# MLA queries of a two-layer decoder step in six projection tiles instead of eight, with the rotary halves in tiles of their own

## The chip, the cores and the metric

One program on 1 core of a Trainium2 chip. The metric is device microseconds of that core for the whole step, both layers; lower is better.

## The reference

One inference step of a two-layer decoder for 256 prompt tokens (one sequence) and 64 sample tokens (8 sequences of 8, each with 2048 cached positions). All is kept feature-major: 128 features on the partitions, the 320 tokens along the row. Per layer:

```
x += 0.5 * SwiGLU(RMSNorm(x))
x += W_out [HGRN2 | RWKV-7 | MLA](RMSNorm(x) @ W_in)
x += 0.5 * SwiGLU(RMSNorm(x))
```

The change touches the MLA queries:

```python
q = (rms_norm(qa, W['mla_q_norm'][l]) @ W['mla_wqb'][l]).reshape(B, T, MLA_HEADS, MLA_NOPE + MLA_ROPE)
q_nope = q[..., :MLA_NOPE]                 # 64 of 96 columns of each of 8 heads
q_pe = rope(q[..., MLA_NOPE:], pos)        # 32 columns, two halves of 16:
                                           # [x1*cos - x2*sin, x2*cos + x1*sin]
c = rms_norm(kva, W['mla_kv_norm'][l])
k_pe = rope(kpe[:, :, None, :], pos)[:, :, 0]
# prompt: scores = q_nope . (c wuk) + q_pe . k_pe
# sample: q_lat = einsum('bqhd,rhd->bqhr', q_nope, wuk); scores = q_lat . c_past + q_pe . kpe_past
```

## The kernel before

Every dense product runs in a split form of fp32: a weight block of 128x128 becomes a rounded high part and a remainder, the moving data too, and `dense_steps` (line 396) issues three matmuls of 320 columns for each block (high x high, high x low, low x high). The weights of a mixer come as one stream of blocks, four to a transfer (`raw`, 256 KB, 4 buffers); `block` (line 382) casts the high part on ACT (line 427) and makes the remainder on DVE (line 428), into three pairs of `w` buffers.

In a layer's mixer, `mla_in` (line 641) projects six tiles: three of the query's low rank, one with the rotary key, two of the latent. It squares the query tiles, sums them over the partitions with a matmul against ones, and takes the root on ACT and the reciprocal on DVE (lines 450 and 451): `rq`. Multiplied by the table `cs` of cosines and sines (with 64 rows of ones on top) that is `csq` (line 671). `mla_q` (line 703) then makes one tile of 128 rows for each of 8 heads: 64 plain rows, 32 rotary rows, and the same 32 with their halves swapped. Two DVE operations take a tile out of PSUM times `csq`: `qS` (64 sample columns, line 721) and `qT` (256 prompt columns, line 722). The matmul over 128 rows then adds rotary and swapped rows by itself, since the key stands twice in `kpe` and `kT`; for the samples line 731 adds them. `absorb` (line 711) multiplies a head's 64 plain rows by `wukt`, three matmuls of 64 columns, and ACT copies the result into `qlat` (line 716), which the sample scores read.

PSUM has 8 banks under four names with a fixed number of buffers each, taken in turn:

```python
BANKS = {"pd": 2, "pr": 3, "pa": 2, "pv": 1}
for h in range(NH):
    ps = self.bank(("pd", "pr", "pr", "pd", "pr")[h % 5])[:, :T]
```

The order of the instructions on each engine comes from the framework's scheduler, which lays the program out by a model of time; `high_priority` moves a part forward. After the queries the mixer weaves three streams (RWKV and HGRN2 recurrences, the attention over cached pages, dense tiles) by a running estimate of TensorE's time. Page tiles (`ct`, `cn`) are fetched on SP's queue, between the weight transfers.

Of the kernel before, what the change touches and what calls it, by code (L numbers as in the profile page):

```python
# [25 lines left out]
NH = 8  # L26
# [72 lines left out]

# [30 lines left out]
def _constants():  # L130
# [11 lines left out]
    r["cs"] = np.concatenate([np.ones((64, T), f), c, c, -s, s], 0).astype(f)  # L142
# [60 lines left out]
def _pack(i):  # L203
# [16 lines left out]
    a["wukt"] = np.concatenate([wukt, np.zeros_like(wukt[..., :32])], 3).reshape(L, 64, NH * 3 * KR)  # L220
# [36 lines left out]
class Kern:  # L257
# [383 lines left out]
    def mla_in(self, xh, xl):  # L641
        nc, l = self.nc, self.l
        self.mark(f"mla_in{l}")
        cs = self.a([128, T], "cs")
        self.wukt = self.a([64, NH, 3 * KR], "wukt")
# [7 lines left out]
        with self.tc.issue_after(self.raws[-1]):  # L653
            nc.sync.dma_start(cs, self.ap["cs"])
# [5 lines left out]
        for j in range(6):  # L660
# [5 lines left out]
            if j == 4:  # L666
                pq = self.bank("pa")[:, :T]
                self.mm(pq, self.c("ones"), accq, start=True, stop=True)
                rq = self.rstd_from(pq, self.ta, "rq", 1.0 / 384)
                self.csq = self.a([128, T], "csq")  # L670
                nc.vector.tensor_tensor(out=self.csq, in0=cs, in1=rq, op=ALU.mult)
            if j < 3:
                qa = self.a([128, T], "qa")
                nc.vector.tensor_tensor(out=qa, in0=ps, in1=self.rstd, op=ALU.mult)
                self.sumsq(qa, accq, j == 0)
                self.split_scaled(qa, self.v(l, "gq", j), self.qh[:, j, :], self.ql[:, j, :])
            elif j == 3:
                csr = self.a([128, T], "qa")
                nc.vector.tensor_tensor(out=csr, in0=cs, in1=self.rstd, op=ALU.mult)
# [3 lines left out]
                for r in (64, 96):  # L683
                    nc.vector.tensor_tensor(out=self.kpe[r:r + 32], in0=t1[64:96], in1=t1[96:128], op=ALU.add)
# [6 lines left out]
    def mla_c(self):  # L691
# [3 lines left out]
        rk = self.rstd_from(ps[:, :T], self.ta, "rq", 1.0 / 256)  # L695
# [7 lines left out]
    def mla_q(self):  # L703


        nc = self.nc
        self.mark(f"mla_q{self.l}")
        self.qT = self.b([128, NH, TP], "qT")
        q = self.a([128, NH, TS], "qS")

        def absorb(h):
            pl = self.bank("pa")
            for kt in range(3):
                self.mm(pl[:KR, kt * 64:kt * 64 + 64], self.wukt[:, h, kt * KR:kt * KR + KR], q[0:64, h, :],
                        start=True, stop=True)
            nc.scalar.copy(self.qlat[:KR, :, :, h, :], pl[:KR, :192].rearrange("p (r s t) -> p r s t", r=3, t=8))

        for h in range(NH):
            ps = self.bank(("pd", "pr", "pr", "pd", "pr")[h % 5])[:, :T]
            self.dense(ps, 3, self.tiles(self.qh, 3), self.tiles(self.ql, 3))  # L720
            nc.vector.tensor_tensor(out=q[:, h, :], in0=ps[:, TP:], in1=self.csq[:, TP:], op=ALU.mult)
            nc.vector.tensor_tensor(out=self.qT[:, h, :], in0=ps[:, :TP], in1=self.csq[:, :TP], op=ALU.mult)
            if h == 4:
                self.mla_c()
            if h > 1:
                absorb(h - 2)
        absorb(6)
        absorb(7)

        sp = lambda x: x.rearrange("p h (s t) -> p s h t", t=8)  # L730
        nc.vector.tensor_tensor(out=self.qlat[64:96, 2], in0=sp(q[64:96]), in1=sp(q[96:128]), op=ALU.add)


    def prompt(self):
# [9 lines left out]
        kT = self.b([128, NH, TP], "kT")  # L744
        for h in range(0, NH, 4):
            nc.gpsimd.tensor_copy(kT[64:128, h:h + 4, :], self.kpe[64:128, None, :TP].to_broadcast([64, 4, TP]))
# [788 lines left out]
```

## Time and profile before

| what | value |
|---|---|
| median of 3 runs | 1675.93 us (1675.06 to 1678.35) |
| the profiled execution's own time | 1670.47 us |
| its span, first to last instruction | 1668.5 us |
| PE busy | 1625.2 us, 97% of the span |
| DVE busy | 955.0 us, 57% |
| ACT busy | 716.6 us, 43% |
| POOL busy | 80.2 us, 5% |
| mean granted TensorE clock | 0.988 |
| bytes moved by DMA | 260.05 MB, mean 156 GB/s |

PE's matmuls are pipelined, so a row of the timeline is longer than the distance to the next row; what a matmul costs in a row of its kind is that distance. A bracket at the end of a timeline row is the idle time before it and what ended it. In the first layer the MLA part lies at 250 to 294 us, in the second at 1073 to 1116 us.

### The profile page before, as it was taken

The numbers are of one execution on the slowest core, as the hardware profiler recorded it, in microseconds if no ns is written. First come the engines' busy times: TensorE is split into PE (matmuls) and PEld (weight loads), VectorE is DVE, ScalarE is ACT, GpSimd is POOL, SyncE is SP. The second block draws the span as 40 slices with busy tenths as digits, with TensorE's granted clock in tenths as the row PEclk, the third lists the DMA queues.
The fourth block names the chain that finished last, engine by engine and source line by source line (L and its number), as shares of the span: only waits on it lengthen the run. The fifth ranks groups of instructions, "written<-read, shape, count | busy, mean of one in ns | idle before, by whom it ended". The sixth has DMA issues, their size and how long they took to land.

```text
span 1668.5 us, 33401 instructions
## 1 busy us (share of the span) xinstructions
PE 1625.2 (97%) x13174; PEld 1449.8 (87%) x13174; DVE 955.0 (57%) x1599; ACT 716.6 (43%) x1208; POOL 80.2 (5%) x112
## 2 busy tenths in 40 slices
PE   8999999999989899999999999999999999999998
PEld 8999998777657599999999999987766676999997
DVE  7555447854446585554465554478335565755543
ACT  6444334633343364443344443346233543544432
POOL 0000000200022000000000000002000310000000
PEclk9999999999999999999999999999999999999999
DMA  8555526646564465555545555366357644555442
GB/s 282 152 150 147 149 86 170 184 143 180 155 209 138 133 209 152 152 152 149 148 146 152 152 151 148 105 175 189 109 157 208 189 134 132 159 152 150 149 148 91
DMA packets 130908, 260.05 MB, mean 156 GB/s; under 512 B 17264, under 2 KB 75952, under 8 KB 130624
## 3 DMA queue, kind: packets, MB, share of 16 engines
q1 hardware_dynamic: 119072, 237.21, 48.0%
q10 hardware_dynamic: 11648, 20.65, 4.1%
q8 instruction: 104, 1.70, 0.4%
q0 software_dynamic: 32, 0.07, 0.1%
q14 instruction: 52, 0.43, 0.1%
HBM read 253.39 MB, written 4.47 MB: 155 GB/s over the span
## 4 chain that ended last, share of the span: by engine, by line
PE 65%; DVE 2%; DMA 2%; ACT 1%; SPq 1%; issue 1%; DVEq 0%; ACTq 0%
PE pd L286 25%; PE pr L286 23%; PE pa L286 14%; PE pv L286 3%; PE pa L290 1%; DMA cn<-in_cn 1%; ACT S L903 0%; DMA ct<-in_ct 0%; DVE w L428 0%; DMA raw<-in_wm 0%; SPq L874 0%; PE pd L290 0%; SPq L917 0%; SPq L854 0%; ACT L903 0%
## 5 line engine op out<-in xcount | busy, mean ns | idle before, releaser
L428 DVE TENSOR_TENSOR w<-raw,w 128x1024 fp32r<-128x1024 f32 (+1 forms) x392 | 410.9, 1051 | 321.4 <-ACT w L427 308.9
L427 ACT CAST w<-raw 128x1024 fp32r<-128x1024 f32 (+1 forms) x392 | 354.7, 909 | 425.0 <-PE pd L286 203.1
L286 PE MATMUL pd<-xh,w 128*128 128x320 f32 x1792 | 425.2, 316 | 7.7 <-ACT w L427 6.8
L286 PEld LDWEIGHTS pd<-xh,w 128*128 128x128 f32 x1792 | 305.6, 190 | 24.2 <-issue 9.7
L286 PE MATMUL pd<-xl,w 128*128 128x320 f32 x896 | 280.1, 314 | 0.0
L286 PE MATMUL pr<-xh,w 128*128 128x320 f32 x1056 | 240.2, 310 | 0.0
L286 PE MATMUL pa<-xh,w 128*128 128x320 f32 x896 | 201.7, 309 | 0.0
L286 PEld LDWEIGHTS pr<-xh,w 128*128 128x128 f32 x1056 | 178.3, 188 | 0.5
L286 PEld LDWEIGHTS pd<-xl,w 128*128 128x128 f32 x896 | 169.7, 189 | 2.9 <-issue 0.9
L286 PE MATMUL pr<-xl,w 128*128 128x320 f32 x528 | 162.5, 309 | 0.0
L286 PE MATMUL pd<-hh,w 128*128 128x320 f32 x704 | 158.2, 309 | 0.0
L286 PE MATMUL pr<-hh,w 128*128 128x320 f32 x704 | 158.2, 309 | 0.0
L286 PEld LDWEIGHTS pa<-xh,w 128*128 128x128 f32 x896 | 151.0, 188 | 0.0
L286 PE MATMUL pa<-xl,w 128*128 128x320 f32 x448 | 137.6, 309 | 0.0
L286 PE MATMUL pa<-ct,qlat 96*64 96x256 f32 x768 | 125.1, 398 | 3.9 <-DMA ct<-in_ct 3.9
L286 PEld LDWEIGHTS pr<-hh,w 128*128 128x128 f32 x704 | 118.5, 188 | 0.0
L286 PEld LDWEIGHTS pd<-hh,w 128*128 128x128 f32 x704 | 118.5, 188 | 0.0
L286 PE MATMUL pd<-hl,w 128*128 128x320 f32 x352 | 108.8, 309 | 0.0
L286 PE MATMUL pr<-hl,w 128*128 128x320 f32 x352 | 108.8, 309 | 0.0
L286 PEld LDWEIGHTS pr<-xl,w 128*128 128x128 f32 x528 | 99.1, 188 | 0.3
L475 ACT ACTIVATE fa<-fa 128x320 f32<-128x320 f32 x88 | 41.4, 472 | 134.7 <-DVE fa L474 134.7
L286 PEld LDWEIGHTS pa<-ct,qlat 96*64 96x64 f32 x768 | 59.2, 139 | 40.5 <-issue 13.5
(381 smaller groups left out, 2011.0 us busy)
## 6 DMA issues: line engine op xcount, KB each, us to landing
raw<-in_wf SPq DMA_DIRECT2D x264, 512.0 KB, 3.6
ct<-in_ct SPq DMA_DIRECT2D x256, 144.0 KB, 2.8
cn<-in_cn SPq DMA_DIRECT2D x256, 128.0 KB, 2.4
raw<-in_wm ACTq DMA_DIRECT2D x76, 256.0 KB, 3.3
raw<-in_wm SPq DMA_DIRECT2D x52, 256.0 KB, 3.7
xT<-in_x SPq DMA_DIRECT2D x4, 320.0 KB, 6.7
wukt<-in_wukt SPq DMA_DIRECT2D x2, 576.0 KB, 6.1
S<-in_rws SPq DMA_DIRECT2D x4, 256.0 KB, 3.4
```

The lines of the kernel that those rows point to most:

```text
L286: self.last = self.nc.tensor.matmul(out, w, x, start=start, stop=stop)
L290: self.nc.tensor.transpose(out, x, ident)
L427: self.cast = nc.scalar.copy(h, src).ins
L428: nc.vector.tensor_tensor(out=lo, in0=src, in1=h.bitcast(F32), op=ALU.subtract)
L475: nc.scalar.activation(a, a, AF.Silu)
```

## The change

The 64 plain columns of two heads fill one tile, so eight heads take four tiles (index `g`); the first rotary halves of all heads (8 x 16 = 128 rows) are a fifth tile, the second halves a sixth. The six tiles are issued with the rotary pair first. From the two rotary tiles in PSUM, DVE makes four products with cosine and sine (`y`, `z`), GpSimd subtracts or adds them, and four SBUF-to-SBUF transfers on ACT's queue carry the 16-row pieces of each head to rows 64 to 95 of `qT` and of a new tile `qR`; a DVE copy puts `qR` into `qlat`. The plain tiles are taken out times `rq` alone. The tables grow to three (`cs`, 128x960), of which two are multiplied by `rq` in place on GpSimd. `wukt` has two heads on the two halves of the partitions (128x1152 where it was 64x2304), so that `absorb` reads rows 0 to 63 or 64 to 127. The query norm is computed in the step of the third query tile, and that part has high priority. Where rows of queries and keys were 128, they are 96, and the rotary key stands once. Two blocks of zeros fill the weight stream up to a multiple of four, and are skipped.

```diff
-            if j == 4:
-                pq = self.bank("pa")[:, :T]
-                self.mm(pq, self.c("ones"), accq, start=True, stop=True)
-                rq = self.rstd_from(pq, self.ta, "rq", 1.0 / 384)
-                self.csq = self.a([128, T], "csq")
-                nc.vector.tensor_tensor(out=self.csq, in0=cs, in1=rq, op=ALU.mult)
...
+                    if j == 2:
+
+                        pq = self.bank("pa")[:, :T]
+                        self.mm(pq, self.c("ones"), accq, start=True, stop=True)
+                        self.rq = self.rstd_from(pq, self.ta, "rq", 1.0 / 384)
+                        self.csq = cs[:, 1:3]
+                        nc.gpsimd.tensor_tensor(out=self.csq, in0=self.csq, in1=self.rq[:, None, :].to_broadcast([128, 2, T]), op=ALU.mult)
...
-                for r in (64, 96):
-                    nc.vector.tensor_tensor(out=self.kpe[r:r + 32], in0=t1[64:96], in1=t1[96:128], op=ALU.add)
+                nc.vector.tensor_tensor(out=self.kpe[64:96], in0=t1[64:96], in1=t1[96:128], op=ALU.add)
...
-        self.qT = self.b([128, NH, TP], "qT")
-        q = self.a([128, NH, TS], "qS")
...
-        for h in range(NH):
-            ps = self.bank(("pd", "pr", "pr", "pd", "pr")[h % 5])[:, :T]
-            self.dense(ps, 3, self.tiles(self.qh, 3), self.tiles(self.ql, 3))
-            nc.vector.tensor_tensor(out=q[:, h, :], in0=ps[:, TP:], in1=self.csq[:, TP:], op=ALU.mult)
-            nc.vector.tensor_tensor(out=self.qT[:, h, :], in0=ps[:, :TP], in1=self.csq[:, :TP], op=ALU.mult)
...
+        V, x = nc.vector, [self.bank(n)[:, :T] for n in ("pd", "pr")]
+        y, z = self.a([128, 2, T], "y"), self.a([128, 2, T], "z")
+        for i in range(2):
+            self.dense(x[i], 3, qh, ql)
+        for i in range(2):
+            V.tensor_tensor(out=y[:, i], in0=x[i], in1=self.csq[:, 0], op=ALU.mult)
+            V.tensor_tensor(out=z[:, i], in0=x[1 - i], in1=self.csq[:, 1], op=ALU.mult)
+            nc.gpsimd.tensor_tensor(out=y[:, i], in0=y[:, i], in1=z[:, i], op=ALU.add if i else ALU.subtract)
+            r = slice(64 + 16 * i, 80 + 16 * i)
+            nc.scalar.dma_start(qr[r], y[:, i, TP:])
+            nc.scalar.dma_start(qT[r], y[:, i, :TP])
+
+        def absorb(g):
+            for hh, r in enumerate(R2):
+                pl = self.bank("pa")
+                for kt in range(3):
+                    self.mm(pl[:KR, kt * 64:kt * 64 + 64], self.wukt[r, g, kt * KR:kt * KR + KR], q[r, g, :], start=True, stop=True)
+                nc.scalar.copy(self.qlat[:KR, :, :, 2 * g + hh, :], pl[:KR, :192].rearrange("p (r s t) -> p r s t", r=3, t=8))
+
+        for g in range(4):
+            ps = self.bank(("pd", "pr", "pr", "pd")[g])[:, :T]
+            self.dense(ps, 3, qh, ql)
+            V.tensor_tensor(out=q[:, g, :], in0=ps[:, TP:], in1=self.rq[:, TP:], op=ALU.mult)
+            for hh, r in enumerate(R2):
+                V.tensor_tensor(out=qT[0:64, 2 * g + hh, :], in0=ps[r, :TP], in1=self.rq[r, :TP], op=ALU.mult)
+            if g == 2:
+                self.mla_c()
+            if g:
+                absorb(g - 1)
+        absorb(3)
+        self.st["wm"][1] += QPAD
...
-        nc.vector.tensor_tensor(out=self.qlat[64:96, 2], in0=sp(q[64:96]), in1=sp(q[96:128]), op=ALU.add)
+        V.tensor_copy(self.qlat[64:KR, 2], qr[64:KR].rearrange("p h (s t) -> p s h t", t=8))
```

On DVE in the first layer, from the reciprocal of the query norm on, the order before (numbers behind a name tell tiles of one name apart; `w` is the remainder of a weight transfer):

```order
L451 RECIPROCAL rq_2662<-rq_2662 128x320
L428 TENSOR_TENSOR w_415_2792<-raw_2789,w_414_2791 128x512
L428 TENSOR_TENSOR w_422_2828<-raw_2825,w_421_2827 128x512
L671 TENSOR_TENSOR csq_2665<-cs_2435,rq_2662 128x320
L428 TENSOR_TENSOR w_427_2854<-raw_2851,w_426_2853 128x512
L721 TENSOR_TENSOR qS_2711<-pd_2712,csq_2665 128x64
L722 TENSOR_TENSOR qT_2710<-pd_2712,csq_2665 128x256
L721 TENSOR_TENSOR qS_2711<-pr_2730,csq_2665 128x64
L722 TENSOR_TENSOR qT_2710<-pr_2730,csq_2665 128x256
```

and with the change, where line numbers are those of the changed file:

```order
L458 RECIPROCAL rq_2581<-rq_2581 128x320
L435 TENSOR_TENSOR w_417_2801<-raw_2798,w_416_2800 128x512
L435 TENSOR_TENSOR w_425_2843<-raw_2840,w_424_2842 128x512
L742 TENSOR_TENSOR qS_2709<-pd_2755,rq_2581 128x64
L744 TENSOR_TENSOR qT_2708<-pd_2755,rq_2581 64x256 x2
L742 TENSOR_TENSOR qS_2709<-pr_2774,rq_2581 128x64
L744 TENSOR_TENSOR qT_2708<-pr_2774,rq_2581 64x256 x2
L435 TENSOR_TENSOR w_443_2896<-raw_2893,w_442_2895 128x512
L725 TENSOR_TENSOR y_2713<-pd_2711,cs_2435 128x320
L726 TENSOR_TENSOR z_2714<-pr_2712,cs_2435 128x320
L725 TENSOR_TENSOR y_2713<-pr_2712,cs_2435 128x320
L726 TENSOR_TENSOR z_2714<-pd_2711,cs_2435 128x320
```

The two remainders now follow each other, two plain tiles come out ahead of the rotary pair, and the bank `pd_2711` is read for the last time at the end of the four products.

On PE in the first layer, around the first `absorb`, before (`pd_2821` is the tile of head 5):

```order
L286 MATMUL pr_2788<-ql_2438,w_414_2791 128x320
L286 MATMUL pr_2788<-qh_2437,w_415_2792 128x320
L286 MATMUL pa_2766<-qS_2711,wukt_2436 96x64 x3
L286 MATMUL pd_2821<-qh_2437,w_414_2791 128x320
L286 MATMUL pd_2821<-ql_2438,w_414_2791 128x320
```

and with the change:

```order
L293 MATMUL pr_2797<-ql_2438,w_416_2800 128x320
L293 MATMUL pr_2797<-qh_2437,w_417_2801 128x320
L293 MATMUL pa_2787<-qS_2709,wukt_2436 96x64 x3
L293 MATMUL pa_2792<-qS_2709,wukt_2436 96x64 x3
L293 MATMUL pd_2836<-qh_2437,w_416_2800 128x320
L293 MATMUL pd_2836<-ql_2438,w_416_2800 128x320
```

Before, one `absorb` stood between two tiles, and none followed another directly. Now the fourth plain tile, `pd_2836`, follows two `absorb` groups at once; with two buffers of `pd` it takes the buffer of `pd_2711`, the first rotary tile.

On ACT in the first layer, where the four transfers are issued with the change:

```order
L457 ACTIVATE rk_2818<-pa_2816,eps_102 128x320
L737 COPY qlat_2430<-pa_2826 96x24x8
L729 DMA qR_2710<-y_2713 16x8x64
L730 DMA qT_2708<-y_2713 16x8x256
L729 DMA qR_2710<-y_2713 16x8x64
L730 DMA qT_2708<-y_2713 16x8x256
L737 COPY qlat_2430<-pa_2831 96x24x8
L434 CAST w_453_2959<-raw_2957 128x512
```

Nothing of this stood there before; a copy, a cast and the next weight transfers are queued behind them.

## Rows read from the trace of the kernel before

**Rows 1.** Windows by stage: length, busy us (instructions) of each engine, PEclk, DMA share, GB/s

```profile
580.00:1070.00 490.00, 489.97 (x3340) 488.93 (x3339) 282.61 (x399) 213.20 (x287) 0.00 (x0) 1.00 0.51 149
1116.00:1410.00 294.00, 282.05 (x2990) 198.25 (x2990) 163.32 (x337) 122.31 (x269) 36.93 (x50) 0.98 0.55 161
```

**Rows 2.** PE's timeline in the second layer's queries: start, length, operation, idle before

```profile
1096.21 0.56 PE L286 MATMUL pr<-qh,w 128*128 128x320 f32 x2 [1.44 <-DVE w L428]
...
1098.06 0.72 PE L286 MATMUL pa<-qS,wukt 64*96 64x64 f32 x6 [0.56 <-DVE qS L721]
...
1104.56 0.72 PE L286 MATMUL pa<-qS,wukt 64*96 64x64 f32 x6
```

**Rows 3.** PE's timeline in the first layer's queries

```profile
272.53 0.56 PE L286 MATMUL pr<-qh,w 128*128 128x320 f32 x2 [1.09 <-DVE w L428]
...
274.38 0.72 PE L286 MATMUL pa<-qS,wukt 64*96 64x64 f32 x6 [0.56 <-DVE qS L721]
...
282.12 0.31 PE L286 MATMUL pd<-xl,w 128*128 128x320 f32 x1
282.36 0.72 PE L286 MATMUL pa<-qS,wukt 64*96 64x64 f32 x6
283.00 0.56 PE L286 MATMUL pd<-xh,w 128*128 128x320 f32 x2
283.40 0.31 PE L286 MATMUL pd<-xl,w 128*128 128x320 f32 x1
```

**Rows 4.** DVE's timeline in the second layer's MLA part

```profile
1084.61 0.48 DVE L674 TENSOR_TENSOR qa<-pd,rstd 128x320 f32<-128x320 f32 x1
1085.01 0.68 DVE L428 TENSOR_TENSOR w<-raw,w 128x512 fp32r<-128x512 f32 x1
...
1092.41 1.01 DVE L684 TENSOR_TENSOR kpe<-rt 32x320 f32<-32x320 f32 x2
1093.45 2.15 DVE L451 RECIPROCAL rq<-rq 128x320 f32<-128x320 f32 x1
1095.52 1.23 DVE L428 TENSOR_TENSOR w<-raw,w 128x512 fp32r<-128x512 f32 x2
...
1097.78 0.22 DVE L721 TENSOR_TENSOR qS<-pd,csq 128x64 f32<-128x64 f32 x1
1097.93 0.41 DVE L722 TENSOR_TENSOR qT<-pd,csq 128x256 f32<-128x256 f32 x1
1098.26 0.21 DVE L721 TENSOR_TENSOR qS<-pr,csq 128x64 f32<-128x64 f32 x1
```

**Rows 5.** POOL's groups of instructions: busy us, mean ns of one, idle before

```profile
L1436 POOL TENSOR_TENSOR S<-S,wc 128x512 f32<-128x512 f32 x4 | 4.2, 1042 | 15.3 <-PE pr L286 15.3
```

**Rows 6.** POOL's timeline in the second layer's RWKV part

```profile
1137.12 1.04 POOL L1055 TENSOR_TENSOR bxb<-bxb,sw 128x320 f32<-128x320 f32 x1 [2.29 <-DVE bxb L1054]
...
1157.09 2.65 POOL L1099 COPY rwa<-cf 128x320 f32<-128x320 f32 x1 [7.60 <-DVE bk L1065]
```

**Rows 7.** DVE's timeline around the first of these

```profile
1136.96 0.47 DVE L1018 TENSOR_TENSOR rwv<-pe 128x320 f32<-128x320 f32 x1
1137.34 1.37 DVE L428 TENSOR_TENSOR w<-raw,w 128x512 fp32r<-128x512 f32 x1
```

**Rows 8.** Windows behind the waits of both layers (columns of rows 1)

```profile
275.00:278.00 3.00, 3.00 (x13) 2.64 (x11) 2.37 (x10) 0.94 (x2) 0.00 (x0) 0.50 0.34 102
...
1098.00:1102.00 4.00, 3.94 (x28) 3.62 (x29) 3.25 (x13) 1.33 (x4) 0.00 (x0) 1.00 0.53 162
```

**Rows 9.** Windows at the start of the second layer's mixer (columns of rows 1)

```profile
1076.00:1080.00 4.00, 4.00 (x30) 4.00 (x28) 3.00 (x4) 2.31 (x3) 0.00 (x0) 1.00 0.96 206
1080.00:1084.00 4.00, 3.92 (x26) 3.42 (x25) 2.12 (x5) 1.96 (x4) 0.00 (x0) 1.00 1.06 323
```

**Rows 10.** ACT's timeline there

```profile
1082.01 0.62 ACT L427 CAST w<-raw 128x512 fp32r<-128x512 f32 x1 [3.69 <-DMA raw<-in_wm]
```

**Rows 11.** DMA issues on ACT's queue: KB each, median us from issue to landing

```profile
raw<-in_wm ACTq DMA_DIRECT2D x76, 256.0 KB, 3.3
```

More of the change, by code (lines that the diff above doesn't have):

```diff
@@ L141, in _constants @@
     c, s = np.cos(ang), np.sin(ang)
-    r["cs"] = np.concatenate([np.ones((64, T), f), c, c, -s, s], 0).astype(f)
+    r["cs"] = np.concatenate([np.concatenate([c, c, -s, s] * 2, 0), np.repeat(c, 8, 0), np.repeat(s, 8, 0)], 1).astype(f)
     r["pidx"] = (t[:, None] + np.arange(L)[None, :] * NPOOL * KR).astype(f)
@@ L219, in _pack @@
     wukt = wuk.transpose(0, 3, 2, 1)[..., KORD]
-    a["wukt"] = np.concatenate([wukt, np.zeros_like(wukt[..., :32])], 3).reshape(L, 64, NH * 3 * KR)
+    wukt = np.concatenate([wukt, np.zeros_like(wukt[..., :32])], 3)
+    a["wukt"] = wukt.reshape(L, 64, 4, 2, 3 * KR).transpose(0, 3, 1, 2, 4).reshape(L, 128, 12 * KR)
     a["hgs0"] = i["state_hgrn"].reshape(L, 8, 2, 2, 64, 64).transpose(0, 3, 4, 2, 1, 5).reshape(L, 128, 1024)
@@ L628, in idx_setup @@
         self.qlat = self.m([128, 3, 8, NH, 8], "qlat")
-        self.kpe = self.m([128, T], "kpe")
+        self.kpe = self.m([KR, T], "kpe")
     def sumsq(self, src, acc, first):
@@ L643, in mla_in @@
         self.mark(f"mla_in{l}")
-        cs = self.a([128, T], "cs")
-        self.wukt = self.a([64, NH, 3 * KR], "wukt")
+        cs = self.a([128, 3, T], "cs")
+        self.wukt = self.a([128, 4, 3 * KR], "wukt")
         self.qh = self.a([128, 3, T], "qh", dt=F32R)
@@ L665, in mla_in @@
                 self.dense(ps, KD, xh, xl)
[L666 to L676 removed]
+            if j < 3:
+                with self.tc.high_priority(offset=1000):
+                    qa = self.a([128, T], "qa")
+                    nc.vector.tensor_tensor(out=qa, in0=ps, in1=self.rstd, op=ALU.mult)
+                    self.sumsq(qa, accq, j == 0)
+                    self.split_scaled(qa, self.v(l, "gq", j), self.qh[:, j, :], self.ql[:, j, :])
+                    if j == 2:
[4 more added lines that the diff above has]
+                        nc.gpsimd.tensor_tensor(out=self.csq, in0=self.csq, in1=self.rq[:, None, :].to_broadcast([128, 2, T]), op=ALU.mult)
             elif j == 3:
                 csr = self.a([128, T], "qa")
[L679 removed]
+                nc.vector.tensor_tensor(out=csr[64:], in0=cs[64:, 0], in1=self.rstd[64:], op=ALU.mult)
                 t1 = self.a([128, T], "rt1")
                 nc.vector.tensor_tensor(out=t1[64:], in0=ps[64:], in1=csr[64:], op=ALU.mult)
[L683 to L684 removed]
+                nc.vector.tensor_tensor(out=self.kpe[64:96], in0=t1[64:96], in1=t1[96:128], op=ALU.add)
                 nc.sync.dma_start(self.ap["o_kpe"][l], self.kpe[64:96, :])
@@ L707, in mla_q @@
         self.mark(f"mla_q{self.l}")
-        self.qT = self.b([128, NH, TP], "qT")
-        q = self.a([128, NH, TS], "qS")
[L711 to L716, printed above, removed]
-        for h in range(NH):
-            ps = self.bank(("pd", "pr", "pr", "pd", "pr")[h % 5])[:, :T]
-            self.dense(ps, 3, self.tiles(self.qh, 3), self.tiles(self.ql, 3))
-            nc.vector.tensor_tensor(out=q[:, h, :], in0=ps[:, TP:], in1=self.csq[:, TP:], op=ALU.mult)
-            nc.vector.tensor_tensor(out=self.qT[:, h, :], in0=ps[:, :TP], in1=self.csq[:, :TP], op=ALU.mult)
-            if h == 4:
-                self.mla_c()
-            if h > 1:
-                absorb(h - 2)
@@ L727, in mla_q @@
-        absorb(6)
-        absorb(7)
-        sp = lambda x: x.rearrange("p h (s t) -> p s h t", t=8)
-        nc.vector.tensor_tensor(out=self.qlat[64:96, 2], in0=sp(q[64:96]), in1=sp(q[96:128]), op=ALU.add)
+        qT = self.qT = self.b([KR, NH, TP], "qT")
+        q = self.a([128, 4, TS], "qS")
+        qr = self.a([KR, NH, TS], "qR")
+        qh, ql = self.tiles(self.qh, 3), self.tiles(self.ql, 3)
+        V, x = nc.vector, [self.bank(n)[:, :T] for n in ("pd", "pr")]
+        y, z = self.a([128, 2, T], "y"), self.a([128, 2, T], "z")
@@ L743, in prompt @@
         V = self.b([128, 2, 512], "V")
[L744 removed]
+        kT = self.b([KR, NH, TP], "kT")
         for h in range(0, NH, 4):
[L746 removed]
+            nc.gpsimd.tensor_copy(kT[64:KR, h:h + 4, :], self.kpe[64:KR, None, :TP].to_broadcast([32, 4, TP]))
         sums = self.t(self.xp, [128, 4, 8], "acc")
```

10 lines of the change are left out of this document (6 added, 4 removed).

## The prediction

> **What bounds the kernel now.** I read the windows by stage first. In the gate and output layers between the two mixers PE is busy 489.97 of 490 us with 3340 matmuls [rows 1]: PE never waits there, and a dense matmul of 320 columns costs 490 / 3340 = 0.147 us. So a matmul taken from PE is worth its time, unless a wait takes its place. In the second layer's woven part PE idles 294 - 282.05 = 12 us [rows 1]; page loads and short recurrences end those waits, and what comes before only shifts them. Then I read the timelines of the MLA part, where all of the change lies. PE stops twice in each layer there: 1.09 and 1.44 us for the remainder `w` of a weight transfer, then 0.56 us each for the first `qS` [rows 2, 3]. DVE's timeline says why: the reciprocal of the query norm takes 2.15 us, two remainders stand behind it in order, and the outputs of the tiles behind these [rows 4]. In this stretch DVE is thus the late engine, and its order decides.
>
> **What goes from PE.** Two tiles of three blocks with three matmuls: 18 x 0.147 = 2.64 us a layer. The 24 short matmuls of `absorb` stay, but their eight groups now stand in five places. Going into such a group and out of it costs about 0.1 us each: 282.12 to 282.36 is 0.24 where a dense step is 0.147, and the two steps of 283.00 to 283.40 take 0.40 instead of 0.29 [rows 3]. Three places fewer: 0.6 us. One weight transfer a layer goes too, with its cast and remainder; neither is late at that point, so I count nothing. The old waits go as such, 1.65 and 2.00 us, and new ones are counted in full below.
>
> **What DVE and POOL do to PE's waits.** I follow the second layer, which ran at full clock.
>
> First wait: one addition for the key falls away ahead of the reciprocal, half of 1.04 us [rows 4]. The reciprocal starts 0.52 earlier, the first remainder is ready 0.52 earlier, and PE resumes at 1095.69: 0.92 us of wait are left, in the first layer 0.57.
>
> Second wait: as soon as the reciprocal is out, POOL multiplies two tables by it, 640 elements in a row. Before there is no such operation; 512 elements take 1.04 us [rows 5], so 640 take an estimated 1.3. From below the bound is nothing, if it runs beside free work; from above it is the slowest row, a copy of 320 elements in 2.65 us [rows 6], or 5.3 for 640. I take 1.3, since the operation is of the kind of rows 5. The rows also show what it does to DVE. At 1137.12 a POOL operation on SBUF starts while DVE subtracts two SBUF tensors (`pe`); DVE's next operation, a remainder, then takes 1.37 us [rows 7] where the pair of remainders takes 1.23 [rows 4], and ends at 1138.71, 0.55 behind POOL's end at 1138.16. The same neighbours meet here: remainder, POOL's product, remainder. So POOL runs from the first remainder's end, 1095.7, to 1097.0, and the second remainder ends at 1097.55. The Trainium skill (SBUF — State Buffer, Who interferes with whom) says that a DVE instruction with two SBUF inputs and a GpSimd instruction that reads SBUF exclude each other for a whole instruction; by that rule the 1.37 us are a wait for POOL, and the trace agrees.
> The first `qS` is then out at 1097.7. PE, with seven dense steps and a change of kind after 1095.69, is there at 1096.8: 0.9 us of wait in each layer.
>
> Third wait, a new one: the fourth plain tile takes the PSUM buffer of the first rotary tile, which is free only after the last of four products. DVE takes out two plain tiles first, 0.15 + 2 x 0.33 us each by the distances of `qS` and `qT` [rows 4] (half as many rows at the same row length: same time), to 1099.1; a remainder, 0.61, to 1099.7; then four products of 320 columns at 0.40 distance and 0.48 length, as `qa` [rows 4], to 1101.4. PE has finished both `absorb` groups by 1097.7 + 2 x 0.64 + 0.2 = 1099.2 and waits 2.2 us.
>
> Sum of a layer, second: -2.64 - 0.6 - 2.00 + 0.92 + 0.9 + 2.2 = -1.2; first: -2.64 - 0.6 - 1.65 + 0.57 + 0.9 + 2.2 = -1.2. Both: -2.4 us.
>
> **The clock.** Behind 1.65 us of waits in the first layer the granted clock was 0.50, the lower of the two levels, from 275 to 278; behind 2.00 us in the second it stayed at 1.00 [rows 8]. The same work, from the first `absorb` group to the third, took 282.36 - 274.38 = 7.98 us there and 1104.56 - 1098.06 = 6.50 here [rows 2, 3]: a drop costs 1.5 us. With the change each layer idles 3.7 to 4.0 us in the same stretch, so I count a drop in both, one more than before: +1.5. Bounds: none in either (-1.5), two each (+4.5).
>
> **What I cost at nothing.** The table load grows by 320 KB a layer ahead of weights that ACT already awaits: 3.69 us at 1082.01 [rows 10]. At 323 GB/s [rows 9] that is 1.0 us later at worst. But `wukt` (576 KB) goes from 64 to 128 partitions, and the stretch in which it is carried moves only 206 GB/s at a DMA share of 0.96, where 323 are reached later [rows 9]: at the better rate it would save 2.8 - 1.8 = 1.0 us. I take 0 between +1.0 and -1.0. The Trainium skill (SBUF — State Buffer, Door 1: The DMA port swizzle) says that 64 partitions reach only 8 of 16 ports; no run here has `wukt` alone. The four SBUF transfers land a few us after POOL's sums, by 3.3 us for 256 KB [rows 11] some 4 us after issue, around 1108; their reader, the copy into `qlat`, stands behind the dense tiles as line 731 did, close to 1114. Six us cover them. ACT holds 4 issues there with casts behind, several us ahead of their use. A scheduler that lays out a changed program shifts the woven part too: its waits, 12 us in a layer, may change by some tenths each way; I allow 2.5 us in all.
>
> **The forecast** is thus -2.4 + 1.5 = -0.9 us: against the profiled execution 1670.47 - 0.9 = 1669.6. The median of the runs shown lies 5.5 us above that execution, so I apply the difference to it: 1675.93 - 0.9 = **1675.0 us**. No change that a measurement can tell: 0.2% is 3.4 us.
>
> **The rivals.**
> - *POOL gives way.* The second remainder goes first. Then `qS` is ready at 1096.5, ahead of PE, and the products end at 1100.1: only 1.8 us of wait there, where PE comes at 1098.3. A layer gains 2.64 + 0.6 + 2.00 - 0.92 - 1.8 = 2.5, both 5.0, with the clock as before: 1670.9; with one more drop 1672.4. For it: in rows 6 the copy of 2.65 us had been passed by DVE's operations. Against it: rows 7. Chance 0.25.
> - *POOL is slow* (the other side). At 5.3 us the product ends 4.0 us later, the second remainder, both plain tiles and the four products wait behind it in order, and PE with them: +8.0 - 0.9 = +7.1, 1683.0. It is slower by more than 0.2% from 3.4 us for the product on: (3.4 + 0.9) / 2 = 2.1 above 1.3. For it: the 2.65 us of rows 6. Against it: few operations with two SBUF inputs surround it here. Chance 0.1.
> - *The halves overlap.* If two heads on different halves of the array ran together, six of a pair's twelve steps would vanish: 0.64 us each for the three pairs behind the third wait (the first only waits longer), 3.8 in both layers, 1671.2. Against it: each head's three matmuls are issued in a run, so the halves do not alternate. The Trainium skill (TensorE: Matmul & The Clock Gate, Part 3: Packing small matmuls) says that matmuls at different tile positions run concurrently; no row here shows it for this shape. Chance 0.05.
> - *The weights come late*: +1.0 a layer, 1677.0. Against it: `wukt` above. Chance 0.1.
>
> My own case has 0.5.
>
> **How the numbers follow.** Own case: with 2.5 us of new order about -0.9, 0.10 faster, 0.36 same, 0.04 slower. POOL gives way: 0.16 faster, 0.09 same. POOL slow: 0.09 slower, 0.01 same. Overlap: 0.04 and 0.01. Late weights: 0.08 same, 0.02 slower. Together 0.30, 0.55, 0.15. The range leaves out slow POOL and reaches from the first rival with some luck in the new order, 1669.5, to late weights with a bad one, 1680.0.
>
> **What would show it.** On PE in each layer three waits, about 0.6 to 0.9 for `w`, 0.9 for `qS`, 2.2 for a product `z`, then a granted clock of 0.50; on DVE the second remainder behind the reciprocal at 1.8 us or more; on POOL 1.3 us for `cs`. No wait for `qS` and a remainder of 0.6 us is the first rival; a POOL row above 3 us the second; 18 short steps closer than 0.1 us the third; a longer wait of ACT for `raw` near 1082 the last. I am wrong in kind if PE's third wait is missing, or if the mixers' woven parts move by more than the MLA parts.

## The result, and the profile after

| | before | with the change |
|---|---|---|
| median, first comparison | 1677.14 us (4 runs) | 1661.14 us (4 runs, 1657.07 to 1663.59) |
| ratio, 95% interval | | 0.992 (0.989 to 0.995) |
| the same two kernels once more | 1673.12 us (15 runs) | 1661.27 us (5 runs), 0.993 (0.991 to 0.996) |
| the profiled execution | 1670.47 us, clock 0.988 | 1657.07 us, clock 0.993 |

Forecast were 1675.0 us and a range of 1669.5 to 1680.0. The changed kernel is 12 to 16 us (0.7 to 0.8%) faster, and its time lies below the range.

PE's timeline with the change, second layer, then first layer; they answer to [rows 2, 3]:

```profile
1092.66 0.56 PE L293 MATMUL pr<-qh,w 128*128 128x320 f32 x2 [0.99 <-DVE w L435]
1094.88 1.38 PE L293 MATMUL pa<-qS,wukt 64*96 64x64 f32 x12 [0.92 <-DVE qS L742]
1096.19 0.63 PE L293 MATMUL pd<-qh,w 128*128 128x320 f32 x1
...
1099.97 0.41 PE L293 MATMUL pd<-xh,w 128*128 128x320 f32 x1
```

```profile
273.21 0.56 PE L293 MATMUL pr<-qh,w 128*128 128x320 f32 x2 [1.13 <-DVE w L435]
...
275.42 1.15 PE L293 MATMUL pa<-qS,wukt 64*96 64x64 f32 x12 [0.92 <-DVE qS L742]
...
279.88 0.72 PE L293 MATMUL pa<-qS,wukt 64*96 64x64 f32 x6
280.53 0.41 PE L293 MATMUL pd<-xh,w 128*128 128x320 f32 x1
...
282.77 0.94 PE L293 MATMUL pa<-qS,wukt 64*96 64x64 f32 x12
...
283.64 0.56 PE L293 MATMUL pd<-xh,w 128*128 128x320 f32 x2
```

The first two waits are there. The third is not: the row at 1096.19 is the fourth plain tile, and it starts right behind the two `absorb` groups.

DVE's timeline with the change, second layer (answers to [rows 4]), and POOL's:

```profile
1089.91 2.15 DVE L458 RECIPROCAL rq<-rq 128x320 f32<-128x320 f32 x1
1091.98 2.59 DVE L435 TENSOR_TENSOR w<-raw,w 128x512 fp32r<-128x512 f32 x2
1094.60 0.22 DVE L742 TENSOR_TENSOR qS<-pd,rq 128x64 f32<-128x64 f32 x1
1094.74 0.84 DVE L744 TENSOR_TENSOR qT<-pd,rq 64x256 f32<-64x256 f32 x2
...
1098.56 0.48 DVE L726 TENSOR_TENSOR z<-pd,cs 128x320 f32<-128x320 f32 x1
```

```profile
1092.19 1.83 POOL L685 TENSOR_TENSOR cs<-cs,rq 128x640 f32<-128x640 f32 x1 [556.07 <-DVE rq L458]
1098.39 1.68 POOL L727 TENSOR_TENSOR y<-y,z 128x320 f32<-128x320 f32 x2 [4.37 <-DVE z L726]
```

The pair of remainders takes 2.59 us instead of 1.23. The second ends at 1094.57, 0.55 behind POOL's end at 1094.02, the same 0.55 as in [rows 6, 7].

Where did the time go? I cut each layer at ACT's instructions: the MLA part from the first square `accq` to the first decay `sw`, the woven part from there to the first split `xh` of the residual `xT` after it. MLA: 45.9 and 44.7 us before, 42.6 and 43.7 after. Woven, in the windows between these cuts (before, then after):

```profile
305.07:588.74 283.67, 271.32 (x2935) 191.06 (x2936) 157.76 (x324) 116.01 (x261) 35.79 (x42) 0.98 0.54 159
1127.27:1413.36 286.09, 274.13 (x2935) 193.01 (x2936) 157.84 (x324) 117.75 (x262) 35.54 (x42) 0.98 0.54 158
```

```profile
302.43:586.13 283.70, 274.11 (x2930) 192.07 (x2931) 158.37 (x326) 117.01 (x262) 34.20 (x43) 0.98 0.54 159
1123.18:1400.11 276.93, 266.64 (x2928) 186.66 (x2928) 159.31 (x326) 117.24 (x262) 34.17 (x43) 1.00 0.55 163
```

The MLA parts give 3.3 and 1.0 us, the first woven part nothing, the second 9.2 us. The dense layers between the mixers are unchanged [rows 1]:

```profile
580.00:1070.00 490.00, 489.98 (x3338) 489.42 (x3338) 281.74 (x397) 213.15 (x287) 0.00 (x0) 1.00 0.49 150
```

So most of the gain of this profile lies in code that the change does not touch. The granted clock (PEclk, the last column but two) went with it: 0.98 before and 1.00 after in the second woven part. Near its end PE waits for a cached page, before and after:

```profile
1396.35 0.65 PE L286 MATMUL pv<-cn,PT 128*64 128x256 f32 x2 [1.60 <-DMA cn<-in_cn]
...
1397.00:1405.00 8.00, 6.95 (x48) 5.20 (x50) 1.75 (x6) 1.37 (x5) 0.00 (x0) 0.57 0.00 0
```

```profile
1385.20 0.65 PE L293 MATMUL pv<-cn,PT 128*64 128x256 f32 x2 [0.55 <-DMA cn<-in_cn]
...
1385.00:1390.00 5.00, 3.67 (x34) 2.21 (x34) 1.35 (x4) 0.87 (x4) 0.00 (x0) 1.00 0.02 3
```

Behind 1.60 us of wait the granted clock fell to the lower level, behind 0.55 it did not. That does not show the shorter wait to be the reason. A second profile of the changed kernel (after_again) has nearly the same wait at the same place, and there the clock fell:

```profile
1384.44 0.65 PE L293 MATMUL pv<-cn,PT 128*64 128x256 f32 x2 [0.66 <-DMA cn<-in_cn]
...
1389.00:1395.00 6.00, 6.00 (x31) 4.66 (x30) 1.94 (x5) 1.04 (x3) 0.00 (x0) 0.50 0.06 6
```

I count such drops as the sum of (1 - granted clock) over windows of 1 us; one costs 1.7 us by this sum, two in a row 3.4. Before has 6.8 us of them in each woven part, after 5.1 and 0.0. Without them the woven parts take 276.8 and 279.3 us before, 278.6 and 276.9 after: the same in sum.

### The profile page after: what moved, and what is told of

Its sections match the earlier page's. It is cut to its first block, busy times and chain, and to the rows that moved or that the text cites. A ratio compares the mean times of both kernels' runs of the same rounds, so it can differ in the third digit from the quotient of the medians.

```text
span 1655.1 us, 33369 instructions
## 1 busy us (share of the span) xinstructions
PE 1615.0 (98%) x13138; PEld 1441.2 (87%) x13138; DVE 957.8 (58%) x1593; ACT 716.0 (43%) x1207; POOL 83.6 (5%) x118
## 4 chain that ended last, share of the span: by engine, by line
PE 88%; DVE 5%; ACT 3%; DMA 2%; issue 1%; SPq 1%; ACTq 0%; DVEq 0%
PE pd L293 33%; PE pr L293 31%; PE pa L293 18%; PE pv L293 4%; DVE w L435 1%; PE pa L297 1%; ACT S L924 1%; DMA cn<-in_cn 1%; DMA raw<-in_wm 1%; DMA ct<-in_ct 1%; DMA xT<-in_x 0%; DVE kS L458 0%; ACT w L434 0%; DVE rt L1073 0%; ACT L924 0%
```

## The experiments

Woven parts and drops (first and second layer), PE's idle time in both together (length less PE's busy time), medians of the time and of the clock over a kernel's runs. Each ratio is against runs of the kernel before made beside it, whose medians lay between 1672.4 and 1677.3 us:

| kernel | woven us | drops us | PE idle us | median us | ratio (95%) | clock |
|---|---|---|---|---|---|---|
| before | 283.7, 286.1 | 6.8, 6.8 | 24.3 | | | 0.986 |
| before_again | 285.1, 290.9 | 8.5, 13.7 | 22.6 | 1672.4 | 1.000 (0.998 to 1.002) | 0.9875 |
| before_relaid | 295.0, 295.5 | 13.7, 10.2 | 34.6 | 1696.7 | 1.015 (1.013 to 1.018) | 0.9805 |
| before_relaid_norm | 281.4, 284.7 | 1.7, 6.8 | 22.6 | 1663.3 | 0.994 (0.992 to 0.997) | 0.9905 |
| before_relaid_copy | 281.2, 287.9 | 5.1, 10.2 | 24.2 | 1670.2 | 0.999 (0.997 to 1.002) | 0.9865 |
| two_tiles_less | 285.9, 299.5 | 10.2, 11.9 | 28.9 | 1685.9 | 1.009 (1.006 to 1.012) | 0.9815 |
| after | 283.7, 276.9 | 5.1, 0.0 | 19.9 | 1661.1 | 0.992 (0.989 to 0.995) | 0.991 |
| after_again | 283.3, 281.3 | 5.1, 5.1 | 20.6 | 1661.3 | 0.993 (0.991 to 0.996) | 0.991 |
| norm_late | 284.4, 282.5 | 6.8, 6.8 | 19.2 | 1662.8 | 0.993 (0.991 to 0.996) | 0.990 |
| after_relaid | 286.4, 297.6 | 5.1, 11.9 | 34.4 | 1678.9 | 1.001 (0.999 to 1.004) | 0.986 |
| after_relaid_bank | 285.8, 281.0 | 5.1, 3.4 | 21.2 | 1659.0 | 0.991 (0.988 to 0.994) | 0.990 |
| after_relaid_copy | 295.2, 295.7 | 11.9, 11.9 | 34.9 | 1686.3 | 1.007 (1.005 to 1.009) | 0.982 |
| csq_dve | 279.3, 283.4 | 3.4, 8.5 | 20.6 | 1655.1 | 0.990 (0.987 to 0.992) | 0.9915 |
| csq_dve_later | 289.7, 293.9 | 8.5, 6.8 | 27.3 | 1675.0 | 1.001 (1.000 to 1.003) | 0.987 |
| csq_dve_alternate | 279.2, 282.6 | 3.4, 6.8 | 20.8 | 1654.6 | 0.991 (0.988 to 0.994) | 0.991 |
| same_half | 285.1, 282.8 | 6.8, 6.8 | 20.2 | 1663.8 | 0.994 (0.992 to 0.997) | 0.9895 |
| before_pinned | 296.3, 295.0 | 4.8, 6.7 | 31.8 | 1695.2 | 1.012 (1.009 to 1.016) | 0.9825 |
| after_pinned | 300.7, 299.0 | 8.5, 11.9 | 32.5 | 1694.9 | 1.012 (1.008 to 1.016) | 0.979 |

**The same kernels again.**

> The kernel before, unchanged, profiled a second time. Stages are cut at ACT's instructions: the MLA part from the first square of the query (accq) to the first decay (sw), the woven part from there to the first split xh after it. Before: MLA 45.9 and 44.7 us, woven 283.7 and 286.1. Theory ORDER (a program's layout fixes its woven parts): 283.7 and 286.1 again, each within 2 us. Theory CLOCK (drops of the granted clock that fall by chance from run to run): one of them moves by 3 us or more, with a drop more or less, about 1.5 us each. Time against before 0.998 to 1.002 by both.

> The changed kernel, unchanged, profiled a second time (first profile: MLA 42.6 and 43.7 us, woven 283.7 and 276.9). ORDER: woven 283.7 and 276.9 again, each within 2 us; time 0.990 to 0.993 of before. CLOCK: the second woven part is nearer to the first, 280 to 284, and the time 0.993 to 0.997.

Both theories caught a part. Within one kernel the second woven part moved by 4 to 5 us with its drops (6.8 to 13.7, 0.0 to 5.1); without drops it held: 279.3 and 277.3 before, 276.9 and 276.2 after. The 9.2 us that the first profile shows there are thus in part luck: the changed kernel's order of the second woven part stands in five more traces (after_again, norm_late, same_half, csq_dve, csq_dve_alternate), and they have 5.1 to 8.5 us of drops where the first has none.

With drops taken out, both layers and both profiles give this account: MLA parts 88.9 and 89.5 us before, 82.9 and 85.4 after; woven parts 556.1 and 553.8 before, 555.5 and 554.3 after. So the MLA parts give some 5 us and the woven parts nothing. All drops in the span are 19.2 and 25.7 us before, 12.0 and 13.3 after: some 10 us. The two add up to the 15 us by which the four profiled spans differ on average.

The runs without a profile agree. The two kernels keep different clocks: 0.979 to 0.991 over all 95 runs of the kernel before beside these experiments, 0.990 to 0.993 over 9 of the changed one. Over the 95 runs the span falls by 1.4 us for each 0.001 of clock. Read from such lines at a clock of 0.990, the spans are 1666.4 before and 1660.9 and 1662.2 after: some 5 us at equal clock, and 0.005 of clock (medians 0.986 and 0.991) is the other 7.

**The norm where it was.**

```diff
-                with self.tc.high_priority(offset=1000):
...
-                    if j == 2:
-                        pq = self.bank("pa")[:, :T]
...
+            if j == 4:
+                pq = self.bank("pa")[:, :T]
...
```

> The changed kernel with the query norm where it was before (in the step of the fifth tile, no raised priority). PE's order is the same as the changed kernel's in every row. ORDER: woven 283.7 and 276.9 within 2 us, as the order is the same, and the MLA parts 0.5 to 1 us longer a layer since the reciprocal comes 0.5 us later (one addition for the key ahead of it again); time 0.991 to 0.994 of before. Theory NORM (the early norm frees DVE and is the gain): the MLA parts are over 2 us longer a layer, time 0.995 to 1.0.

PE's order is the same, and the time too: 1662.8. The early norm by itself brings nothing that can be measured: NORM fell. ORDER's 276.9 for the second woven part did not come either (282.5, with 6.8 us of drops), but without drops the woven parts are the changed kernel's, 277.6 and 275.7.

**Two tiles left out of the kernel before.**

```diff
         for h in range(NH):
-            ps = self.bank(("pd", "pr", "pr", "pd", "pr")[h % 5])[:, :T]
-            self.dense(ps, 3, self.tiles(self.qh, 3), self.tiles(self.ql, 3))
+            if h < 6:
+                ps = self.bank(("pd", "pr", "pr", "pd", "pr")[h % 5])[:, :T]
+                self.dense(ps, 3, self.tiles(self.qh, 3), self.tiles(self.ql, 3))
...
+        self.st["wm"][1] += 6
```

> The kernel before with the matmuls of the last two query tiles left out, and one weight transfer with them (heads 6 and 7 take the numbers of head 5); DVE, ACT, absorb and the tables as before, no rotary tiles, no transfers, no product on POOL. The framework lays its woven parts out anew, in yet another order. Removed work alone is 2.64 us a layer. ORDER: the woven parts leave 283.7 and 286.1 by 2 us or more in at least one layer; the time is anywhere from 0.990 to 0.999. Theory QUERIES (the new tiles themselves ease the woven parts: 96 rows instead of 128, one copy of the key): woven parts as before within 2 us, MLA parts 2.5 to 4 us shorter, time 0.995 to 0.998.

5.3 us of matmuls less, and 13 us slower. The woven parts moved as ORDER said, but its range for the time held only faster results, so that was missed; QUERIES fell. The second woven part is 9 to 13 us longer than in the two profiles of the kernel before, in an order that nobody chose.

**One small re-lay of each kernel.**

```diff
-        nc.vector.tensor_tensor(out=self.qlat[64:96, 2], in0=sp(q[64:96]), in1=sp(q[96:128]), op=ALU.add)
+        nc.vector.tensor_tensor(out=q[64:96], in0=q[64:96], in1=q[96:128], op=ALU.add)
+        nc.vector.tensor_copy(self.qlat[64:96, 2], sp(q[64:96]))
```

> The kernel before with one DVE copy more: the sum of rotary and swapped rows is written in place, and a copy takes it into qlat. The MLA part's PE order moves by 2 rows, the framework lays the woven parts out anew (some 440 and 720 rows of difference in the two layers). Before, two profiles: MLA without clock drops 44.2 to 45.0 us, woven without drops 276.6 to 279.3, drops 6.8 and 8.5 us in the first woven part, 6.8 and 13.7 in the second. ORDER: the sum of drops and woven idle moves by 3 us or more in some layer, and the time leaves 0.998 to 1.002, either way. Theory QUERIES (the gain is tied to the new tiles): the woven parts and drops stay as before and the time at 0.998 to 1.002.

```diff
-            if g == 2:
+            if g == 3:
                 self.mla_c()
```

> The changed kernel with the key norm (mla_c) one tile later: same work, woven parts laid out anew (some 1180 and 750 rows of difference). The changed kernel's drops in the woven parts: 5.1 and 0.0 us in one profile, 5.1 and 5.1 in the other; time 0.992 of before. ORDER: the drops move by 3 us or more, time anywhere from 0.985 to 1.0. QUERIES: drops 5 to 10 us in all, time 0.990 to 0.995.

With a copy of 0.42 us the kernel before is 22 us slower, and moving the key norm by one tile takes back the whole gain: QUERIES fell twice, ORDER held in the drops, with a time (1.001) just above its range for the second. In before_relaid PE's timeline shows what such an order costs:

```profile
1412.18 1.48 PE L286 MATMUL pv<-cn,PT 128*64 128x256 f32 x8 [2.16 <-DMA cn<-in_cn]
1414.17 0.65 PE L286 MATMUL pv<-cn,PT 128*64 128x256 f32 x4 [0.50 <-DMA cn<-in_cn]
1416.88 0.65 PE L286 MATMUL pv<-cn,PT 128*64 128x256 f32 x2 [2.06 <-DMA cn<-in_cn]
```

By the brackets of both woven parts, PE waits 11.1 us for `cn` pages there, 4.8 and 4.4 in the two profiles before, 3.2 and 5.3 after. So this wait tells before_relaid from before, but not before from after. There the wait for the other pages, `ct`, differs (3.9 and 3.5 before, 0.6 and 0.6 after), without making the woven parts shorter at full clock.

**csq on DVE.**

```diff
-                        nc.gpsimd.tensor_tensor(out=self.csq, in0=self.csq, in1=self.rq[:, None, :].to_broadcast([128, 2, T]), op=ALU.mult)
+                        nc.vector.tensor_tensor(out=self.csq, in0=self.csq, in1=self.rq[:, None, :].to_broadcast([128, 2, T]), op=ALU.mult)
```

> The changed kernel with the product csq (640 columns) on DVE instead of POOL, behind the same two remainders. Theory PORT (POOL's 1.83 us holds up the second remainder, which makes qS late): the pair of remainders takes 1.23 to 1.3 us instead of 2.59, csq 0.8 us, and PE's wait for qS falls from 0.92 to 0.2 to 0.4 us in each layer. Rival: the second remainder is late for its own weights; then the pair stays at 2.5 us and the wait grows to 1.7. The second layer's PE order is that of the changed kernel, the first layer's woven part differs in some 500 rows: by ORDER the first woven part may move, the second has drops of 0 to 7 us as in the three profiles of that order. Time 0.989 to 0.994 of before.

DVE's timeline in the second layer, and PE's in the first:

```profile
1085.73 1.22 DVE L435 TENSOR_TENSOR w<-raw,w 128x512 fp32r<-128x512 f32 x2
1086.87 0.82 DVE L685 TENSOR_TENSOR cs<-cs,rq 128x640 f32<-128x640 f32 x1
1087.72 0.22 DVE L742 TENSOR_TENSOR qS<-pd,rq 128x64 f32<-128x64 f32 x1
```

```profile
274.15 0.94 PE L293 MATMUL pa<-qS,wukt 64*96 64x64 f32 x12 [0.30 <-DVE qS L742]
```

PORT holds: the pair is back at 1.22, and the wait for `qS` at 0.30 in both layers. At 1655.1 us (1654.4 to 1656.8, the changed kernel 1657.1 to 1663.7) this is faster than both kernels; 0.6 us a layer of it is shown. The rest lies in the woven parts: without drops the first, in a new order, takes 275.9 us where the changed kernel has 278.6 and 278.1, the second, in the same order, 274.9 where it has 276.9 and 276.2; the latter has no explanation here.

```diff
         for g in range(4):
...
+            if g == 1:
+                V.tensor_tensor(out=self.csq, in0=self.csq, in1=self.rq[:, None, :].to_broadcast([128, 2, T]), op=ALU.mult)
+                for i in range(2):
+                    V.tensor_tensor(out=y[:, i], in0=x[i], in1=self.csq[:, 0], op=ALU.mult)
...
```

> The changed kernel with csq on DVE behind the first plain tile's outputs instead of ahead of them. PORT: no wait of PE for qS in either layer (0.92 in the changed kernel), MLA parts 0.7 to 1.0 us shorter than the changed kernel's 40.9 to 42.9 (without drops). The woven parts are laid out anew (some 320 and 960 rows): by ORDER they may move by 3 us or more either way. Time 0.985 to 0.997 of before.

The four products, POOL's sums and the transfers moved into the loop with it. No wait for `qS` is left and the MLA parts are 37.8 and 39.4 us, 2.6 to 4.8 us shorter than the changed kernel's. That is more than forecast, probably since the cut at `sw` moves with the order. The woven parts take it back (281.2 and 287.1 us without drops): 1675.0 us, 1.001 of before, above the forecast range.

**Woven parts pinned.**

```diff
                 self.mla_q()
+            self.tc.strict_bb_all_engine_barrier()
...
             self.woven = False
+            self.tc.strict_bb_all_engine_barrier()
```

> The kernel before with a barrier of all engines behind the queries of each layer and one behind each woven part, so that the framework lays out a woven part from a fresh start, whatever the MLA part did. Its woven order is new (some 1360 and 850 rows against before), so by ORDER its time is open, 0.995 to 1.02 of before; each barrier costs some us. It is the base for the next kernel.

> The changed kernel with the same barriers. PE's order in its first woven part is that of before_pinned in every row, in the second 84 rows of some 1500 differ. Theory ORDER (the change itself is worth what it does to the MLA parts, and the rest of its gain was the new order of the woven parts with fewer clock drops): the woven parts take the same time in both pinned kernels within 3 us without drops, the MLA parts are 2 to 3.5 us shorter a layer, and the time is 4 to 8 us below before_pinned. Theory QUERIES (the new tiles ease the woven parts themselves): 12 us or more below before_pinned, with woven parts 3 us or more shorter a layer.

1695.19 and 1694.88 us: no difference. Without drops the MLA parts are 2.1 and 2.0 us shorter (40.8 to 38.7 and 38.9), the woven parts 0.6 us longer and 1.2 shorter (291.6 to 292.2, 288.3 to 287.1). The changed kernel has more drops here, in the MLA parts too (6.8 us each against 5.1), and a clock of 0.979 against 0.9825. At a clock of 0.980 and 0.981, where both have runs, its spans are 1692.9 and 1691.2 against 1697.3 and 1694.9: some 4 us apart. So ORDER holds in the stages and at equal clock, but in the time its 4 to 8 us did not come. The barrier also lays bare the end of the MLA part, where the changed kernel waits in both layers for ACT's `rk`:

```profile
1118.18 4.18 PE L293 MATMUL pa<-qS,wukt 64*96 64x64 f32 x30 [3.19 <-ACT rk L457]
```

**Two heads on the two halves.**

```diff
-                    self.mm(pl[:KR, kt * 64:kt * 64 + 64], self.wukt[r, g, kt * KR:kt * KR + KR], q[r, g, :], start=True, stop=True)
+                    self.mm(pl[:KR, kt * 64:kt * 64 + 64], self.wukt[R2[0], g, kt * KR:kt * KR + KR], q[R2[0], g, :], start=True, stop=True)
```

> The changed kernel, but absorb reads rows 0 to 63 of qS and wukt for both heads of a pair (the odd heads take the even heads' numbers). Instructions, order and waits are the changed kernel's. In the changed kernel a pair of absorb groups takes 0.87 us from its first step to the next dense one (282.77 to 283.64), a single one 0.65 (279.88 to 280.53). Theory OVERLAP (matmuls on the two halves run partly at once, so the second head costs 0.22 instead of some 0.43): a pair takes 1.05 to 1.3 us, and the time is 1 to 2.5 us above the changed kernel's 1661. Rival SWITCH (going into and out of a group costs 0.4 us, whatever half): a pair stays at 0.85 to 0.90 us, the time at 1661 within 2.

PE's timeline of same_half, first layer:

```profile
281.12 1.23 PE L293 MATMUL pa<-qS,wukt 64*96 64x64 f32 x12
282.28 0.56 PE L293 MATMUL pd<-xh,w 128*128 128x320 f32 x2
```

A pair takes 1.16 us where the two halves take 0.87: OVERLAP, by 0.29 us. The median is 1663.8, some 2.5 above the changed kernel's, at the edge of the forecast band and within the spread of either, so the time alone shows nothing.

```diff
-            for hh, r in enumerate(R2):
-                pl = self.bank("pa")
-                for kt in range(3):
+            pls = [self.bank("pa") for _ in R2]
+            for kt in range(3):
+                for pl, r in zip(pls, R2):
                     self.mm(pl[:KR, kt * 64:kt * 64 + 64], self.wukt[r, g, kt * KR:kt * KR + KR], q[r, g, :], start=True, stop=True)
+            for hh, pl in enumerate(pls):
```

> csq_dve with the three matmuls of a pair's two heads alternating between the halves, instead of three on one half and then three on the other; order otherwise the same. OVERLAP: a pair takes 0.65 to 0.80 us instead of 0.87, three pairs a layer, so 0.4 to 1.3 us in all, time 1653 to 1656. SWITCH: a pair stays at 0.87 us or takes longer, time 1655 within 2. By ORDER the woven parts, whose order is csq_dve's, keep their 275.9 and 274.9 us without clock drops within 2 us.

```profile
283.67 0.94 PE L293 MATMUL pa<-qS,wukt 64*96 64x64 f32 x12
284.54 0.41 PE L293 MATMUL pd<-xh,w 128*128 128x320 f32 x1
```

The pairs stay at 0.87 us: alternating adds nothing, and OVERLAP's number fell here. 1654.6 us, ratio 0.991 (0.988 to 0.994), as csq_dve.

**Four more re-lays**, two of each kernel, to tell whether the new tiles make better orders (TILES) or whether either kernel may get a good or a bad one (LUCK).

```diff
-            if h == 4:
+            if h == 0:
                 self.mla_c()
```

> The kernel before with the key norm (mla_c) behind the first query tile instead of the fifth: same work, woven parts laid out anew (some 1440 and 1120 rows). By LUCK the time is anywhere from 1660 to 1695, by TILES (only the new tiles give good orders) 1670 or more.

```diff
-            nc.scalar.copy(self.qlat[:KR, :, :, h, :], pl[:KR, :192].rearrange("p (r s t) -> p r s t", r=3, t=8))
+            nc.vector.tensor_copy(self.qlat[:KR, :, :, h, :], pl[:KR, :192].rearrange("p (r s t) -> p r s t", r=3, t=8))
```

> The kernel before with the copies of absorb's results into qlat on DVE instead of ACT: same work on PE, woven parts laid out anew (some 1100 and 650 rows). LUCK: 1660 to 1695. TILES: 1670 or more.

```diff
-            ps = self.bank(("pd", "pr", "pr", "pd")[g])[:, :T]
+            ps = self.bank(("pr", "pd", "pr", "pd")[g])[:, :T]
```

> The changed kernel with another order of PSUM banks for the four plain tiles (pr, pd, pr, pd): same work, woven parts laid out anew (some 160 and 840 rows). LUCK: 1653 to 1690. TILES: 1665 or less.

```diff
-        V.tensor_copy(self.qlat[64:KR, 2], qr[64:KR].rearrange("p h (s t) -> p s h t", t=8))
+        nc.gpsimd.tensor_copy(self.qlat[64:KR, 2], qr[64:KR].rearrange("p h (s t) -> p s h t", t=8))
```

> The changed kernel with the copy of the rotary rows into qlat on POOL instead of DVE: same work on PE, woven parts laid out anew (some 1170 and 920 rows). LUCK: 1653 to 1690. TILES: 1665 or less.

LUCK. A kernel without any new tile reaches 1663.3 us, and one with all of them 1686.3. The four orders of the kernel before (without barriers) span 1663 to 1697 us, those of the changed kernel with `csq` on POOL 1659 to 1686, and they overlap. Four orders of each are too few to exclude that the new tiles make good orders a little more likely; what is shown is that they do not ensure one. In after_relaid_copy the moved copy itself takes 0.60 us on POOL instead of 0.42 on DVE, so it is not the 25 us.

## Why the prediction was wrong

The step that failed is the allowance for the woven parts: "its waits, 12 us in a layer, may change by some tenths each way; I allow 2.5 us in all". It priced their waits alone. "The clock" counted drops only in the queries' stretch, so the drops in the woven parts, 13.7 and 22.2 us in two profiles of the kernel before, were put at nothing. They fell to 5.1 and 10.2 us, and over all runs the clock rose from 0.986 to 0.991, worth 7 us. Both signs that the text had named for being wrong in kind came: PE's third wait is missing, and in the profile the woven parts moved by more than the MLA parts. Point by point:

- **Two tiles and a transfer fewer**: as forecast, -2.64 us a layer.
- **Absorb in five places**: mis-sized. A pair takes 0.87 us and two single groups 2 x 0.65, so three pairs save 1.3 us a layer, not 0.6. Of it, 0.29 each is overlap (same_half). The rival "halves overlap" counted three pairs behind the third wait, where the order has two (the first pair stands ahead of it). Dismissed with 0.05 because the halves do not alternate, it was half right: a run of three on one half followed by three on the other overlaps too. The Trainium skill (TensorE: Matmul & The Clock Gate, Part 3: Packing small matmuls) says that matmuls at different tile positions run at the same time; the trace agrees in part, 0.29 of the 0.51 us (1.16 - 0.65) that the second head costs on the same half.
- **First wait**: 1.13 and 0.99 us, forecast 0.57 and 0.92; after_again has 0.32 and 0.91.
- **Second wait**: 0.92 us in both layers, forecast 0.9. POOL's product took 1.83 us, not 1.3. It started at 1092.19, inside the pair of remainders and not behind the first, which is the likely reason; the pair is 1.37 us longer than in csq_dve. The second remainder ended 0.55 us behind it, as the step said. csq_dve took POOL away, and the wait fell to 0.30. The Trainium skill (SBUF — State Buffer, Who interferes with whom) has the two as exclusive for a whole instruction; 2.59 against 1.22 us agrees.
- **Third wait**: failed. "The fourth plain tile takes the PSUM buffer of the first rotary tile" (and the section on the change with it) took the two `pd` buffers as handed out in turn. The tile starts at 1096.19, while the first rotary tile is still read by `z` at 1098.56; so it has the other of the two buffers, which the first plain tile had left by 1095.58 (1094.74 + 0.84). The wait for `z` goes to the next dense tile, and is smaller. after_again shows it in the second layer:

```profile
1097.68 0.42 PE L293 MATMUL pd<-xh,w 128*128 128x320 f32 x1 [0.57 <-DVE z L726]
```

  That is 2.2 us a layer counted that are 0 to 0.58.
- **The clock in the MLA part**: +1.5 forecast, a drop in each layer. In the first profile that is what happened, in after_again neither layer dropped, though its second layer has nearly the same two waits (0.91 and 0.93 us). So the +1.5 was right once by chance. The second layer of the first profile:

```profile
1096.00:1098.00 2.00, 2.00 (x9) 1.88 (x9) 1.92 (x5) 1.13 (x3) 0.00 (x0) 0.50 0.27 98
```

- **Costed at nothing**: the larger table, `wukt` and the transfers brought no further wait of PE above 0.2 us in the projections and queries, and ACT's wait for `raw` is 3.46 us instead of 3.69 [rows 10]. The rivals of late weights and of a slow POOL (above 3 us) did not come.
- **"I allow 2.5 us in all" for the woven parts**: this is the step that made the forecast wrong. The text knew that a changed program is laid out anew, and gave it some tenths each way, for waits. Re-lays that change next to no work moved whole kernels by -12 to +25 us. With the waits as measured (and none for `z`) my sum would have been -3.5 us in the first layer and -4.0 in the second before clock drops, and with the +1.5 the forecast 1669.9 us; the MLA terms alone do not explain the result. At equal clock some 5 us are seen, in the pinned pair some 4. The other 7 to 11 us of the result are this order's fewer clock drops. From the point of view of the forecast they are luck: of six re-lays of the two kernels three became slower, by 18 to 25 us, and three the same or faster, by 2 to 12.

Not settled: why one order has fewer drops than another. Drops come and go in one and the same order behind nearly the same waits, as the two profiles of the changed kernel show. Nor is PE's idle time the whole reason: the two pinned kernels have nearly the same woven order, with 32 and 33 us of idle time, and still 11.5 and 20.4 us of drops. It is also open why one order brings the `cn` pages 11 us late and another 3 to 5; the runs show that it does, and not which of the scheduler's choices decides it. My sum of -7.5 us (-6.4 with the waits for `z` that after_again has, 0.58 and 0.57 us) and the 5 us seen in the MLA parts differ by 1 to 2.5 us that no run accounts for.

## What to carry to other kernels

Where a scheduler lays out a program by a model of time, a change in one stage re-lays the stages behind it, and that may weigh more than the change: measure two or three neutral re-lays of both kernels before a gain of 1% is put down to the edit, and compare stages, not totals. Read the granted clock with the time, compare spans at equal clock, and take more than one profile: one of them may have the drops that the next has not. A product on GpSimd beside DVE operations with two SBUF inputs was paid by DVE here (1.37 us a layer on the pair of remainders, 0.6 us on PE); DVE did it alone in 0.82 us instead of 1.83.

## What was not expected of the hardware

- Matmuls of 64 rows on the two halves of the array overlap when three on one half are followed by three on the other: 0.87 us for six against 1.16 on one half. Alternating them one by one gains nothing more.
- Time follows the granted clock closely for one and the same program: 95 runs of the kernel before lie between 0.979 and 0.991, 1.4 us of span for each 0.001, and stray from that line by 1.3 us (standard deviation).
- The same program in the same order, with waits at that place alike within 0.11 us, had a drop of 3.4 us in one execution and none in another.
